# Stick-breaking weights by a product scan over keys, and a last output block handled in two pieces

## The chip, the cores and the metric

The kernel runs on one core of a Trainium2 chip. The metric is the device time of one execution in microseconds; lower is better. The engines are named as in the profile: PE is TensorE's matmul (PEld its weight load), DVE is VectorE, ACT is ScalarE, POOL is GpSimd, SP is SyncE, which issues most DMAs.

## The reference

Two layers of a hybrid block over 256 positions and width 1024, then a final RMSNorm. In each layer one projection feeds three branches, whose gated outputs are concatenated, projected and added to the residual:

- eight heads of dilated causal attention with rotary positions (A),
- a convolution and a gated linear recurrence (B),
- four heads of stick-breaking attention (C).

The change is in the third one and in the final norm. For one head and one block of queries:

```python
z = jnp.einsum('bhqd,bhkd->bhqk', q_blk, kf) * scale
causal = key_pos[None, :] < t[:, None]
log_keep = jnp.where(causal, jax.nn.log_sigmoid(-z), 0.0)
tail = lax.cumsum(log_keep, axis=3, reverse=True)
between = jnp.concatenate([tail[..., 1:], jnp.zeros_like(tail[..., :1])], axis=-1)
weights = jnp.where(causal, jnp.exp(jax.nn.log_sigmoid(z) + between), 0.0)
return jnp.einsum('bhqk,bhkd->bhqd', weights, vf)
```

A weight is thus sigmoid(z) of its key times the product of sigmoid(-z) over all later keys that are still before the query. The last step is `rms_norm(h, final_gain)`, where h has 1024 columns.

## The kernel before

All is held on the chip, 128 rows at a time. Weights come in chunks of 2048 columns, in two halves each, through five staging buffers `st`. A float32 number is split into a rounded high part (`whi`, by ACT, L103) and a rest (`wlo`, by DVE, L104), and each product is three matmuls (`mm3`, L207). Four chunks of split weights fit at a time. The order of the chunks is fixed: CH_CQ, CH_CK, CH_AQ[0], CH_AK[0], CH_BX, CH_AQ[1], CH_AK[1], CH_CG, CH_BG, CH_AG, then the output chunks. SP issues a half's DMA when its staging buffer is free, that is, when DVE has split the half that stood five halves ahead.

The instructions of PE stand in the order of the code, which was written out by hand; the other engines' orders are set by a scheduler when the program is built. Each engine runs its queue in order. Small jobs are put between the two column blocks of a projection: `proj_b(chunk, mid)` runs `mid` between them.

Stick-breaking attention before: `sb_scores` (in the middle of CH_AQ[0]) multiplies keys by queries, so that the keys lie on the partitions, with 256 queries for the first 128 keys and 128 for the second. It adds the mask with bfloat16 matmuls (`idb`, `cmb`). For each head, ACT and DVE make log(1 + e^z) from Abs, Exp, Ln, a maximum and a sum, and DVE splits that into `sh` and `sl`. `sb_weights` then sums over later keys with four matmuls a head against a triangular table `trir` (L397, L399), onto the scores themselves, and ACT takes Exp (L82) to `wv`. The four calls of `sb_weights` stand after blocks of CH_AK[0] and CH_BX. With the keys on the partitions, `values` (L358) can use `wv` at once. It writes the bank `y`, of which there is one.

The dilated attention has the queries on the partitions in its scores (L426); its probabilities are turned by PE (`dil_transposes`, L455) and copied by ACT to `wv` (L456). DVE's `emit_y` (L345) frees the `y` bank.

ACT's functions need tables: Exp and Ln are in one set, Sigmoid and Tanh in another, and a change of set is an instruction (L76).

At the end of layer 1, DVE adds each 512-column block of the output to the residual (L588). Then, for each of the two row blocks, ACT squares the two halves with a sum (L189), Ln and Exp give `rstd` (L82), DVE multiplies by the gain (L595), DVE and ACT scale one half each (L597, L599), and SP issues the output (L600).

Of the kernel before, what the change touches and what calls it, by code (L numbers as in the profile page):

```python
# [9 lines left out]
F32 = mybir.dt.float32  # L10
# [5 lines left out]
P = 128  # L16
# [12 lines left out]
AHEAD = 2  # L29
WST = 5  # L30
SCR = 7
WARM = 7

C_ID = 0
C_NM = 128
C_CM = 512
C_TRI = 640
C_W = 768
SM_P = 16
SM_W = 512  # L40
SHUF = list(range(8, 16)) + list(range(0, 8)) + list(range(16, 32))
# [6 lines left out]
def trunk_kernel(ctx: ExitStack, tc: tile.TileContext, x, first_x, first, wpack, prm_d, gatew, gains, consts, rope, out):  # L48
# [15 lines left out]
    def scr(w):  # L64
        return wk.tile([P, 512], F32, name="scr", tag="scr", bufs=SCR)[:, 0:w]

# [5 lines left out]

    loaded = {"load": None, "users": []}

    def table(name):
        load = act.preload_act_table_set(name)  # L76
        for u in loaded["users"]:
            dep(load, u)
        loaded["load"], loaded["users"] = load, []

    def tab(*a, **k):
        i = dep(act.activation(*a, **k), loaded["load"])  # L82
        loaded["users"].append(i)
        return i
# [7 lines left out]
    xh = sb.tile([P, NK, S], F32R, name="xh", tag="xh")  # L92
    xl = sb.tile([P, NK, S], F32R, name="xl", tag="xl")

    def load_chunk(l, c):
        hi = wsp.tile([P, 2048], F32R, name="whi", tag="whi")
        lo = wsp.tile([P, 2048], F32R, name="wlo", tag="wlo")
        for i in range(2):
            st = wst.tile([P, 1024], F32, name="st", tag="st")
            nc.sync.dma_start(out=st, in_=wpack[l, c][:, i * 1024:(i + 1) * 1024])  # L100
            for j in range(0, 1024, 512):
                ws, ss = slice(i * 1024 + j, i * 1024 + j + 512), slice(j, j + 512)
                act.activation(hi[:, ws], st[:, ss], AF.Copy)  # L103
                dve.tensor_sub(lo[:, ws], st[:, ss], hi[:, ws].bitcast(F32))  # L104
        return hi, lo

# [70 lines left out]

    tiny = cst.tile([P, 1], F32, name="tiny")
    dve.memset(tiny, 1e-19)
    trir = cst.tile([P, 2, P], F32R, name="trir")  # L180
    ones = cst.tile([P, P], F32, name="ones")
    dve.memset(ones, 1.0)
    idb = cst.tile([P, P], BF16, name="idb")
# [18 lines left out]
    def mm3(ps, lhs, rhs, ks, first, last):  # L202
        lh, ll = lhs
        rh, rl = rhs
        seq = [(a, b, k) for a, b in ((lh, rh), (lh, rl), (ll, rh)) for k in ks]
        for i, (a, b, k) in enumerate(seq):
            pe.matmul(ps, a(k), b(k), start=first and i == 0, stop=last and i == len(seq) - 1)  # L207

    def normed(t):
        rstd = rms_stats(t, gps)  # L210
# [50 lines left out]
    for l in range(L):  # L261
# [87 lines left out]
        def head(h):  # L349
            return slice((h % 2) * HD, (h % 2) * HD + HD), h // 2, slice(h * HD, (h + 1) * HD)  # L350
# [10 lines left out]

        qc = sb.tile([P, 2, S], F32, name="qc", tag="q1")
        kc = sb.tile([P, 2, S], F32, name="kc", tag="k1")
        zs, sp_hl = {}, {}

        def sb_scores():
            for p in (0, 2):
                for h in (p, p + 1):
                    zs[h] = bank(at, "s")
                for h in (p, p + 1):  # L370
                    hr, hb, _ = head(h)
                    pe.matmul(zs[h][:, 0:256], kc[hr, hb, 0:128], qc[hr, hb, :], start=True, stop=True)  # L372
                for h in (p, p + 1):
                    hr, hb, _ = head(h)
                    pe.matmul(zs[h][:, 256:384], kc[hr, hb, 128:256], qc[hr, hb, 128:256],  # L375
                              start=False, stop=True, skip_group_check=True)
            for h in range(NHC):
                for c in (0, 256):
                    pe.matmul(zs[h][:, c:c + 128], idb, cmb, start=False, stop=True, skip_group_check=True)  # L379
            for h in range(NHC):  # L380
                z = zs[h]
                e = scr(384)
# [3 lines left out]
                sp = scr(384)  # L386
                dve.scalar_tensor_tensor(sp, z[:, 0:384], 0.0, e, ALU.max, ALU.add)
                sh = wk.tile([P, 384], F32R, name="sh", tag="sh", bufs=3)
                sl = wk.tile([P, 384], F32R, name="sl", tag="sl", bufs=3)
                dve.tensor_copy(sh, sp)  # L390
                dve.tensor_sub(sl, sp, sh.bitcast(F32))
                sp_hl[h] = sh, sl

        def sb_weights(h):
            z = zs[h]
            for sv in sp_hl[h]:
                pe.matmul(z[:, 128:256], trir[:, 1, :], sv[:, 256:384], start=False, stop=True,  # L397
                          skip_group_check=True)
                pe.matmul(z[:, 0:384], trir[:, 0, :], sv, start=False, stop=True, skip_group_check=True)  # L399
            if h == 0:  # L400
                zs["w"] = wk.tile([P, 4, 384], F32, name="wv", tag="wv", bufs=1)
            tab(zs["w"][:, h, :], z[:, 0:384], AF.Exp)

        def rotate(ps, tiles, h0, tag):
            dst = tiles[h0] = sb.tile([P, 2, S], F32, name=tag, tag=tag)
# [5 lines left out]
            dve.tensor_mul(v2(sw), v2(sw), ss)  # L411
            dve.tensor_add(dst, dst, v2(sw))

        halves = ((0, slice(0, 128)), (1, slice(128, 384)))
        qT, kT = {}, {}
        prob = {}

# [29 lines left out]
                prob[h] = pr  # L447

        def dil_transposes(h0):
            pts = wk.tile([P, 12, P], F32, name="wv", tag="wv", bufs=1)  # L450
            for g in range(3):
                tp = bank(at, "s")
                for i in range(4):
                    h, j = divmod(4 * g + i, 3)
                    pe.transpose(tp[:, i * P:(i + 1) * P], prob[h0 + h][:, j * P:(j + 1) * P], ident)  # L455
                act.activation(pts[:, 4 * g:4 * g + 4, :].rearrange("p k c -> p (k c)"), tp, AF.Copy)  # L456
            return [pts[:, 3 * h:3 * h + 3, :].rearrange("p k c -> p (k c)") for h in range(4)]
# [49 lines left out]
        if l > 0:  # L507
            scaled(qc, cq_ps, 0.125)
        if l == 0:
            tri = scr(2 * P)  # L510
            nc.sync.dma_start(out=tri, in_=consts[:, C_CM:C_W])
            dve.tensor_copy(idb, ident)
            dve.tensor_copy(cmb, tri[:, 0:P])
            dve.tensor_copy(trir[:, 0, :], tri[:, P:2 * P])
            dve.tensor_scalar(trir[:, 1, :], ones, -1.0, None, ALU.mult)
        ck_ps = proj_b(CH_CK, rows_of_rstd if l == 0 else None)
        if l == 0:
            scaled(qc, cq_ps, 0.125)
# [2 lines left out]
            for i in range(2):  # L521
                dve.tensor_mul(rp0[:, i, :], rp[:, i, :], rb)
        rotate(proj_b(CH_AQ[0], sb_scores), qT, 0, "q0")
        rotate(proj_b(CH_AK[0], lambda: sb_weights(0)), kT, 0, "k0")
        sb_weights(1)
        conv(proj_b(CH_BX, lambda: sb_weights(2)))
        sb_weights(3)
        y_c = {}

        def second():  # L530
            y_c["y"] = values(vc, [zs["w"][:, h, :] for h in range(NHC)], 0)
            dil_softmax(dil_scores(0))

        rotate(proj_b(CH_AQ[1], second), qT, 4, "q1")
# [37 lines left out]
                if (t, n2) == (0, 1):  # L572
                    emit_y(values(va, y_c["p"], 4), ag[:, 2:4, :], 6, 2)
        if l > 0:
            gf = cst.tile([P, D], F32, name="gf", tag="gn")
        nc.sync.dma_start(out=gn if l == 0 else gf, in_=gains[l:l + 1, :].broadcast_to([P, D]))
        ow = [weights(l, CH_O + 2 + n2) for n2 in range(2)]
        for t in range(NT):
            if t == 1 and l == 0:
                next_x = [sb.tile([P, NK, S], F32R, name=n, tag=n) for n in ("xh", "xl")]  # L580
                xn0 = normed(0)
            for n2 in range(2):
                cs = slice(n2 * 512, n2 * 512 + 512)
                for ks in ((0, 1), (2, 3)):
                    out_mm(o_ps[t, n2], ow[n2], t, 1, ks, False, ks[0] == 2)
                    if (l, t, n2, ks[0]) == (0, 1, 1, 0):
                        turn(xn0, 0, *next_x)
                dve.tensor_add(xres[:, t, cs], o_ps[t, n2], xres[:, t, cs])  # L588

    for t in range(NT):  # L590
        rstd = rms_stats(t, gps)
        for half in range(2):
            cs = slice(half * 512, half * 512 + 512)
            ot = scr(512)
            dve.tensor_mul(ot, xres[:, t, cs], gf[:, cs])  # L595
            if half == 0:
                dve.tensor_scalar(ot, ot, rstd, None, ALU.mult)  # L597
            else:
                act.activation(ot, ot, AF.Copy, scale=rstd)  # L599
            nc.sync.dma_start(out=out[t * P:(t + 1) * P, cs], in_=ot)  # L600


def _shape_constants():
    f = np.float32
    con = np.zeros((P, C_W), f)
    con[:, C_ID:C_ID + P] = np.eye(P, dtype=f)
    nm = np.full((P, 384), -8 * BIG, f)
    for t0, c0, n in ((0, 0, 128), (128, 128, 256)):
        d = (t0 + np.arange(P))[:, None] - np.arange(n)[None, :]
        c = (d <= 128).astype(int) + (d % 4 == 0) + (d % 16 == 0)  # L610
        c = np.where(d >= 0, c, 0)
        nm[:, c0:c0 + n] = np.where(c > 0, 8 * np.log(np.maximum(c, 1).astype(np.float64)), -8 * BIG)
# [3 lines left out]
    con[:, C_TRI:C_TRI + P] = np.where(i[:, None] >= i[None, :], -1.0, 0.0)  # L616
    return con


# [89 lines left out]
```

## Time and profile before

| | |
|---|---|
| median of 3 runs | 254.09 us (253.51 to 254.46) |
| the profiled execution | 253.61 us |
| its span | 251.8 us |
| granted TensorE clock, mean | 0.995 |
| mean DMA rate | 173 GB/s |

The profile is of one execution. A row of the groups names line, engine and operation, what is written and read, how often, then busy us in all and mean ns of one, then the engine's idle time just before and what ended it. In a timeline or chain row the first two numbers are the start from the span's beginning and the length, both in us; "x6" says that six instructions are merged. Durations overlap a little on one engine, so starts tell the rate.

### The profile page before, as it was taken

To read this page: it belongs to the slowest core of one execution; us is meant where nothing else is said; L and a number is where in the kernel's file an instruction comes from. 1 tells how busy PE (TensorE), PEld (TensorE's weight loads), DVE (VectorE), ACT (ScalarE), POOL (GpSimd) and SP (SyncE) were. 2 spreads that over 40 slices of the span, in tenths; PEclk is the share of its full clock that TensorE was granted. 3 is DMA by queue.
4 is the path that set the end of the run, shared out by engine and by line. 5 is a ranking of instruction groups with operands and counts; after the bars stand their busy time and mean duration, and the time that the engine had idled before them with its cause. 6 is when DMAs were issued, how large, how long until landed. Compare 5 with 4: busy or idle time off the path is not lost.

```text
span 251.8 us, 4728 instructions
## 1 busy us (share of the span) xinstructions
PE 244.2 (97%) x1777; PEld 223.1 (89%) x1777; DVE 190.7 (76%) x429; ACT 163.9 (65%) x355; POOL 8.3 (3%) x33
## 2 busy tenths in 40 slices
PE   8999999999999999999999999999999999999990
PEld 4989999998999899878889999999899979987870
DVE  4874799999999589985792865399999856985253
ACT  3859969941947499964762864693394659993143
POOL 0037000000000000000000000000000000000000
PEclk9999999999999999999999999999999999999998
DMA  7989988923547631287175586540725732000022
GB/s 215 400 260 407 368 297 272 351 87 99 197 156 235 196 105 64 85 247 275 63 230 189 182 291 198 166 148 21 250 87 163 242 98 83 3 0 0 3 83 83
DMA packets 13126, 43.44 MB, mean 173 GB/s; under 512 B 1584, under 2 KB 2224, under 8 KB 13104
## 3 DMA queue, kind: packets, MB, share of 16 engines
q1 hardware_dynamic: 12816, 42.89, 50.4%
q8 instruction: 14, 0.23, 0.3%
q10 hardware_dynamic: 288, 0.26, 0.3%
q14 instruction: 8, 0.07, 0.1%
HBM read 42.09 MB, written 1.05 MB: 171 GB/s over the span
## 4 chain that ended last, share of the span: by engine, by line
PE 97%; ACT 1%; DVE 0%; issue 0%; ACTq 0%
PE pp L207 66%; PE s L207 9%; PE s L163 5%; PE y L358 3%; PE s L426 2%; PE pp L163 2%; PE s L455 2%; PE s L399 1%; PE pp L481 1%; PE y L134 1%; PE s L372 1%; PE s L223 1%; PE s L379 0%; PE s L397 0%; PE s L375 0%; ACT scr L189 0%
## 5 line engine op out<-in xcount | busy, mean ns | idle before, releaser
L104 DVE TENSOR_TENSOR wlo<-st,whi 128x512 fp32r<-128x512 f32 x132 | 84.5, 685 | 21.9 <-ACT whi L103 21.4
L103 ACT ACTIVATE whi<-st 128x512 fp32r<-128x512 f32 x132 | 74.3, 623 | 35.9 <-PE pp L207 17.2
L207 PE MATMUL pp<-xh,whi 128*128 128x256 f32 x352 | 50.0, 285 | 0.0
L207 PE MATMUL pp<-xl,whi 128*128 128x256 f32 x352 | 49.4, 283 | 0.0
L207 PE MATMUL pp<-xh,wlo 128*128 128x256 f32 x352 | 49.4, 283 | 0.0
L207 PEld LDWEIGHTS pp<-xh,whi 128*128 128x128 f32 x352 | 45.7, 191 | 1.3 <-issue 1.3
L207 PEld LDWEIGHTS pp<-xh,wlo 128*128 128x128 f32 x352 | 45.4, 192 | 0.0
L207 PEld LDWEIGHTS pp<-xl,whi 128*128 128x128 f32 x352 | 45.4, 192 | 0.0
L82 ACT ACTIVATE pr<-scr,mn 128x128 f32<-128x128 f32 (+1 forms) x32 | 14.1, 442 | 9.2 <-DVE mn L433 9.2
L189 ACT ACTIVATE scr<-xres 128x512 f32<-128x512 f32 x12 | 7.5, 627 | 13.4 <-DVE xres L588 12.9
L207 PE MATMUL pp<-whi,yh 128*128 128x512 f32 x48 | 14.1, 394 | 0.0
L207 PE MATMUL pp<-wlo,yh 128*128 128x512 f32 x48 | 13.8, 390 | 0.0
L207 PE MATMUL pp<-whi,yl 128*128 128x512 f32 x48 | 13.8, 389 | 0.0
L76 ACT ACT_TABLE_LOAD x9 | 11.5, 1283 | 1.8 <-PEq L702 1.6
L82 ACT ACTIVATE scr<-scr 128x384 f32<-128x384 f32 (+1 forms) x20 | 10.8, 539 | 0.5 <-DVE scr L324 0.3
L207 PEld LDWEIGHTS pp<-wlo,yh 128*128 128x128 f32 x48 | 9.0, 188 | 1.9
L207 PEld LDWEIGHTS pp<-whi,yl 128*128 128x128 f32 x48 | 9.0, 188 | 1.9
L207 PEld LDWEIGHTS pp<-whi,yh 128*128 128x128 f32 x48 | 8.7, 188 | 1.6
L346 ACT ACTIVATE yh<-scr 128x512 fp32r<-128x512 f32 x8 | 5.1, 633 | 7.6 <-DVE scr L345 7.5
L588 DVE TENSOR_TENSOR xres<-pp,xres 128x512 f32<-128x512 f32 x6 | 4.1, 689 | 7.3 <-PE pp L207 7.3
L433 DVE CUSTOM_DVE_ANT_0 scr<-s,con 128x128 f32<-128x128 f32 (+1 forms) x32 | 9.2, 354 | 0.6 <-PE s L426 0.6
L446 DVE TENSOR_SCALAR pr<-pr,den 128x128 f32<-128x128 f32 (+1 forms) x32 | 8.7, 315 | 0.3
(161 smaller groups left out, 347.5 us busy)
## 6 DMA issues: line engine op xcount, KB each, us to landing
st<-w_pack SPq DMA_DIRECT2D x66, 512.0 KB, 5.1
st<-first SPq DMA_DIRECT2D x7, 512.0 KB, 5.6
xres<-x_in SPq DMA_DIRECT2D x2, 512.0 KB, 8.2
out<-scr SPq DMA_DIRECT2D x4, 256.0 KB, 2.2
gw_t<-gate_w SPq DMA_DIRECT2D x2, 256.0 KB, 6.8
gn<-gains SPq DMA_DIRECT2D x1, 512.0 KB, 6.8
gf<-gains SPq DMA_DIRECT2D x1, 512.0 KB, 4.7
st<-first ACTq DMA_DIRECT2D x2, 128.0 KB, 3.4
```

The source lines that it names most:

```text
L76: load = act.preload_act_table_set(name)
L82: i = dep(act.activation(*a, **k), loaded["load"])
L103: act.activation(hi[:, ws], st[:, ss], AF.Copy)
L104: dve.tensor_sub(lo[:, ws], st[:, ss], hi[:, ws].bitcast(F32))
L163: pe.matmul(ps[t][:, c0 - base:c1 - base], a[:, k, t * P:(t + 1) * P], b[:, c0:c1], start=k == 0 and i == 0 and c0 == base, stop=k == NK - ...
L189: act.activation(scr(512), xres[:, t, i * 512:(i + 1) * 512], AF.Square, accum_out=sq[:, i:i + 1])
L207: pe.matmul(ps, a(k), b(k), start=first and i == 0, stop=last and i == len(seq) - 1)
L346: act.activation(yh[:, k0:k0 + n, :], dst, AF.Copy)
L358: pe.matmul(y[hr, p * 128 + o:p * 128 + 256], vt[:, s0, hs], wts[i][:, ws], start=s0 == 0, stop=s0 == 1)
L426: pe.matmul(sps[h][:, cs], qT[h0][hr, hb, t * P:(t + 1) * P], kT[h0][hr, hb, 0:(t + 1) * P], start=True, stop=True)
L433: dve.tensor_tensor_reduce(xs[:, cs], sps[h][:, cs], nmask[:, cs], -0.125, 3e38, ALU.add, ALU.min, mn[:, t:t + 1])
L446: dve.tensor_scalar(pr[:, cs], pr[:, cs], den[:, t:t + 1], None, ALU.mult)
```

## The change

Scores are made with the queries on the partitions. ACT makes two sigmoids a head, of z and of -z. DVE forms the product over later keys with a scan that runs backward over the keys (two scans a head, one for each block of queries), and multiplies. PE turns the weights in twelve 128 x 128 transposes a layer, in three groups, and ACT copies them to `wv`. The triangular table goes. ACT's table set is changed twice more in each layer. In the last layer, the addition for the last output block is made in two pieces of 320 and 192 columns; DVE sums the squares of the first piece and ACT those of the second; the final norm's steps move into `finish`, called behind each block; and the second half of each output is issued from ACT's queue in place of SP's.

```diff
+LATE = 320
-    def table(name):
+    def table(name, behind=()):
...
-        for u in loaded["users"]:
+        for u in (*loaded["users"], *behind):
...
+    def finish(t, n2):
+        ot = last["ot", t, n2] = scr(512)
+        x_t = xres[:, t, n2 * 512:n2 * 512 + 512]
...
+        if n2 == 0:
+            act.activation(scr(512), x_t, AF.Square, accum_out=sq[:, 0:1])
+            gps.tensor_scalar(ss, sq[:, 0:1], 1.0 / D, EPS, ALU.mult, ALU.add)
+            dve.tensor_mul(ot, x_t, last["gf"][:, 0:512])
+            return
+        c, late = 0, ss
+        if t == 1:
+            c, late = LATE, sq[:, 2:3]
+            dve.tensor_tensor_reduce(scr(c), x_t[:, 0:c], x_t[:, 0:c], 1.0 / D, ss, ALU.mult, ALU.add, late)
+        act.activation(scr(512 - c), x_t[:, c:512], AF.Square, scale=D ** -0.5, accum_out=sq[:, 1:2])
+        dve.tensor_mul(ot, x_t, last["gf"][:, 512:1024])
...
+        for half, queue in ((0, nc.sync), (1, act)):
...
+            queue.dma_start(out=out[t * P:(t + 1) * P, half * 512:half * 512 + 512], in_=o)
...
         def sb_scores():
...
-                    pe.matmul(zs[h][:, 0:256], kc[hr, hb, 0:128], qc[hr, hb, :], start=True, stop=True)
...
+                for t, cs in halves:
+                    for h in (p, p + 1):
+                        hr, hb, _ = head(h)
+                        pe.matmul(zs[h][:, cs], qc[hr, hb, t * P:(t + 1) * P], kc[hr, hb, 0:(t + 1) * P],
+                                  start=t == 0, stop=True, skip_group_check=True)
             for h in range(NHC):
                 for c in (0, 256):
-                    pe.matmul(zs[h][:, c:c + 128], idb, cmb, start=False, stop=True, skip_group_check=True)
+                    pe.matmul(zs[h][:, c:c + 128], cmb, idb, start=False, stop=True, skip_group_check=True)
+            table(SIGM, [split[l, CH_AK[0]]])
             for h in range(NHC):
...
-                act.activation(e, z[:, 0:384], AF.Abs)
-                tab(e, e, AF.Exp, scale=-1.0)
-                tab(e, e, AF.Ln, bias=1.0)
...
+                tab(om, z, AF.Sigmoid, scale=-1.0)
+                tab(bt, z, AF.Sigmoid)
+                w = sw[h] = wk.tile([P, 384], F32, name="sw", tag="sw", bufs=4)
+                gps.memset(w[:, 383:384], 0.0)
+                for lo, k0, k1 in ((0, 1, 128), (127, 128, 384)):
+                    n = k1 - k0
+                    dve.tensor_tensor_scan(w[:, lo:lo + n][:, ::-1], om[:, k0:k1][:, ::-1],
+                                           zero.broadcast_to([P, n]), 1.0, ALU.mult, ALU.add)
+                dve.tensor_mul(w, bt, w)
...
+        def turned(tiles, h0, gs, to):
+            for g in gs:
+                tp = bank(at, "s")
+                for i in range(4):
+                    h, j = divmod(4 * g + i, 3)
+                    pe.transpose(tp[:, i * P:(i + 1) * P], tiles[h0 + h][:, j * P:(j + 1) * P], ident)
+                act.activation(to[:, 4 * g:4 * g + 4, :].rearrange("p k c -> p (k c)"), tp, AF.Copy)
...
-        rotate(proj_b(CH_AK[0], lambda: sb_weights(0)), kT, 0, "k0")
-        sb_weights(1)
-        conv(proj_b(CH_BX, lambda: sb_weights(2)))
-        sb_weights(3)
+        rotate(proj_b(CH_AK[0]), kT, 0, "k0")
+        sw_t = turned_tile()
+        conv(proj_b(CH_BX, lambda: turned(sw, 0, (0,), sw_t)))
+        turned(sw, 0, (1, 2), sw_t)
...
+            table(LN_EXP)
             dil_softmax(dil_scores(0))
...
+                parts = ((0, LATE), (LATE, 512)) if l > 0 and (t, n2) == (1, 1) else ((0, 512),)
```

`split` remembers the last ACT split of each chunk, so that the table load stands behind the splits of CH_AK[0].

The order of instructions moves on three engines. On PE in layer 0, from the projection of CH_AK[0] through CH_BX to CH_AQ[1], each row is eight projection matmuls (L207) or one triangular matmul. Before, at the end of CH_AK[0] and the start of CH_BX:

```order
L207 MATMUL pp<-xh,wlo 128x256 x8
L397 MATMUL s<-sh,trir 128x128
L399 MATMUL s<-sh,trir 128x384
L397 MATMUL s<-sl,trir 128x128
L399 MATMUL s<-sl,trir 128x384
L207 MATMUL pp<-xh,whi 128x256 x8
```

That group stands four times in a layer. In the changed program, CH_BX's two blocks (now L210) and what follows, with the transposes at L433:

```order
L433 MATMUL s<-con,sw 128x128 x4
L210 MATMUL pp<-xh,whi 128x256 x8
L210 MATMUL pp<-xl,whi 128x256 x8
L210 MATMUL pp<-xh,wlo 128x256 x8
L433 MATMUL s<-con,sw 128x128 x8
L210 MATMUL pp<-xh,whi 128x256 x8
```

The four groups of triangular matmuls have become two groups of transposes, in the middle of CH_BX and behind it, and CH_AK[0] runs without a break.

On DVE in layer 0, behind the scores. Before (L387, L390 and L391 are the steps of a head, L104 the splits):

```order
L104 TENSOR_TENSOR wlo<-st,whi 128x512 x7
L387 SCALAR_TENSOR_TENSOR scr<-s,scr 128x384
L104 TENSOR_TENSOR wlo<-st,whi 128x512
L390 CAST sh<-scr 128x384
L104 TENSOR_TENSOR wlo<-st,whi 128x512
L391 TENSOR_TENSOR sl<-scr,sh 128x384
L104 TENSOR_TENSOR wlo<-st,whi 128x512
L387 SCALAR_TENSOR_TENSOR scr<-s,scr 128x384
L104 TENSOR_TENSOR wlo<-st,whi 128x512
```

In the changed program, from the third head's second scan on; L424 is the scans (shown under the name SCALAR_TENSOR_TENSOR), L426 the product, L106 the splits, L447 to L450 the rotation behind CH_AQ[0]:

```order
L424 SCALAR_TENSOR_TENSOR sw<-scr,zero 128x256
L424 SCALAR_TENSOR_TENSOR sw<-scr,zero 128x127
L426 TENSOR_TENSOR sw<-scr,sw 128x384
L424 SCALAR_TENSOR_TENSOR sw<-scr,zero 128x256
L447 STREAM_SHUFFLE scr<-pp 128x512
L426 TENSOR_TENSOR sw<-scr,sw 128x384
L448 TENSOR_TENSOR q_656<-pp,rp_297 128x512
L449 TENSOR_TENSOR scr<-scr,rp_297 128x512
L106 TENSOR_TENSOR wlo<-st,whi 128x512
L450 TENSOR_TENSOR q_656<-q_656,scr 128x512
L106 TENSOR_TENSOR wlo<-st,whi 128x512 x2
```

The splits that stood between the steps of a head now stand behind all four heads' scans; six splits stand directly ahead of the first one.

On ACT in layer 0, from the scores to the first dilated softmax (`pr`). Before, the last three Exp to `wv` and splits:

```order
L82 ACTIVATE wv<-s 128x384
L103 ACTIVATE whi<-st 128x512
L82 ACTIVATE wv<-s 128x384
L103 ACTIVATE whi<-st 128x512 x4
L82 ACTIVATE wv<-s 128x384
L82 ACTIVATE pr,den<-scr,mn 128x128
```

In the changed program, with the sigmoids at L82 and the copies of the turned weights at L434:

```order
L105 ACTIVATE whi<-st 128x512 x12
L76 ACT_TABLE_LOAD
L105 ACTIVATE whi<-st 128x512 x6
L82 ACTIVATE scr<-s 128x384 x8
L105 ACTIVATE whi<-st 128x512 x6
L76 ACT_TABLE_LOAD
L105 ACTIVATE whi<-st 128x512 x4
L434 ACTIVATE wv<-s 128x512
L105 ACTIVATE whi<-st 128x512 x3
L434 ACTIVATE wv<-s 128x512 x2
L105 ACTIVATE whi<-st 128x512
L82 ACTIVATE pr,den<-scr,mn 128x128
```

The second and third copies to `wv` stand behind three of the four splits of CH_BG; before, the last Exp stood behind all four.

More of the change, by code (lines that the diff above doesn't have):

```diff
@@ L385, in sb_scores @@
-                tab(e, e, AF.Ln, bias=1.0)
[L386 to L402, printed above, removed]
+                z = zs[h][:, 0:384]
@@ L404, in rotate, with by_head @@
+        def by_head(pts):
+            return [pts[:, 3 * h:3 * h + 3, :].rearrange("p k c -> p (k c)") for h in range(4)]
         def rotate(ps, tiles, h0, tag):
```

77 lines of the change are left out of this document (36 added, 41 removed).

## The prediction

> **What bounds the kernel now.** I read the page's shares first, then the chain that ended last, then what each engine waited for, and last the timeline around the two changed places.
>
> ```profile
> span 251.8 us, 4728 instructions
> PE 244.2 (97%) x1777; PEld 223.1 (89%) x1777; DVE 190.7 (76%) x429; ACT 163.9 (65%) x355; POOL 8.3 (3%) x33
> ...
> DVE  4874799999999589985792865399999856985253
> ```
>
> The third row is the page's strip of 40 slices.
>
> ```profile
> PE 97%; ACT 1%; DVE 0%; issue 0%; ACTq 0%
> ```
>
> ```profile
> PE y L134 <- DVE cold L122: 1.2, 1, 1.2
> ```
>
> The chain is TensorE for 97% of the span, and the only wait that PE has is the first one, 1.2 us. From there to the last matmul PE never starves, so a matmul taken out before the end moves the end by its whole length, as long as nobody makes PE wait. The strip says where that could happen: VectorE (DVE) has eight nines in a row, from 31 to 82 us, which is layer 0's attention. There it has almost no air, and it feeds PE (splits), SP (freed weight buffers) and the y bank.
>
> **Term 1, PE.** The rows are the chain in order of time (start, length).
>
> ```profile
> 39.62 5.81 PE pp L207 x48
> ...
> 46.00 2.88 PE pp L207 x24
> ...
> 49.45 2.88 PE pp L207 x24
> ...
> 52.90 2.88 PE pp L207 x24
> ...
> 56.34 2.87 PE pp L207 x24
> 59.21 1.45 PE y L358 x16
> ...
> 79.63 1.31 PE s L455 x12
> 80.94 1.73 PE pp L481 x8
> ...
> 159.94 5.81 PE pp L207 x48
> ...
> 179.53 1.45 PE y L358 x16
> ```
>
> From 39.62 to 59.21 are 19.59 us, of which the projections take 5.81 + 3 x 2.88 + 2.87 = 17.32. The four triangular groups between them are the remaining 2.27 us. Layer 1 has the same 19.59 from 159.94 to 179.53, so 4.54 us go in all. What comes is twelve transposes a layer, of the form of L455: twelve stand in 1.31 us. Two layers are 2.62 us. The scores keep their column count, 128 + 256 a head, and the mask keeps its eight matmuls with the operands exchanged, so I count no difference there. Net: 2.62 - 4.54 = -1.92 us, if PE stays fed.
>
> ```profile
> L455 PE MATMUL s<-con,pr 128*128 128x128 f32 x48 | 5.9, 272 | 0.0
> ```
>
> One transpose lasts 272 ns, but they overlap: the chain's row gives 0.109 us each, and I take that. The Trainium skill, TensorE: Matmul & The Clock Gate, Part 4: PE-mode transpose, puts a transpose at about 275 ns in one kernel. Charged like that, 24 would be 6.6 us and the PE term +2.1 us, a loss; this trace has that duration and not that spacing.
>
> **Term 2, DVE and ScalarE (ACT): what has to stay hidden.** Groups by line, with shapes kept apart:
>
> ```profile
> L387 DVE SCALAR_TENSOR_TENSOR scr<-s,scr 128x384 f32<-128x384 f32 x8 | 4.4, 553 | 3.7 <-ACT scr L82 3.7
> L390 DVE CAST sh<-scr 128x384 fp32r<-128x384 f32 x8 | 2.8, 352 | 0.1
> L391 DVE TENSOR_TENSOR sl<-scr,sh 128x384 fp32r<-128x384 f32 x8 | 4.4, 554 | 0.1
> L501 DVE TENSOR_TENSOR_SCAN rt<-av,it 128x256 f32<-128x256 f32 x4 | 2.5, 678 | 0.0
> L522 DVE TENSOR_TENSOR rp<-rp,rb 128x256 f32<-128x256 f32 x2 | 0.8, 418 | 0.0
> L82 ACT ACTIVATE scr<-scr 128x384 f32<-128x384 f32 x16 | 8.3, 519 | 0.3
> L456 ACT ACTIVATE wv<-s 128x512 f32<-128x512 f32 x12 | 6.3, 594 | 1.1 <-PE s L455 1.1
> L76 ACT ACT_TABLE_LOAD x9 | 11.5, 1283 | 1.8 <-PEq L702 1.6
> ```
>
> ```profile
> 37.11 3.69 DVE L104 TENSOR_TENSOR wlo<-st,whi 128x512 fp32r<-128x512 f32 x6
> 96.76 1.27 DVE L501 TENSOR_TENSOR_SCAN rt<-av,it 128x256 f32<-128x256 f32 x2
> ```
>
> Back to back, DVE starts the next instruction about 0.09 us before the old one's end: two scans take 1.27 and not 1.36, six splits 3.69, so 0.60 each. A head costs now 0.47 + 0.27 + 0.47 = 1.21 us of DVE. After: a scan over 256 columns, 0.59; one over 127, which no row shows; and a product over 384, 0.47 (as L391). A 256 scan takes what a 512-wide elementwise takes, so I price the 127 one like a 256-wide elementwise, 0.33 (0.42 less overlap); the ends are 0 and 0.59. No row has a scan through reversed addresses or with a constant second operand; I take the forward price, since that is the same instruction, and the doubled one is a rival below. Sum 1.39, that is 0.18 more a head and 0.72 us more a layer.
>
> ACT loses four activations a head (some 0.5 us each) and gets two sigmoids: eight fewer a layer, 4 us. Three copies and two table loads a layer take that back, 3 x 0.59 + 2 x 1.28 = 4.3 us. It is level, and ACT has a third of its time free. The DVE memset and cast that change, and four memsets of one column on POOL (3% busy), lie under waits.
>
> What is queued behind what is the real question, since the order moves more than the work: all eight scans now stand ahead of the splits that used to stand between the old steps. In layer 0 two chains come close to PE.
>
> (a) There are five staging buffers, so SP issues a half chunk only when DVE has split the one five halves ahead: the second half of CH_BG waits for the second split of CH_AK[1]. Behind the third split of CH_BG stand, on ACT's queue, the last two copies of transposed weights, for which PE's first value products wait.
>
> ```profile
> L100 SPq DMA_DIRECT2D st<-w_pack x1: 327/327/327, 55.8 to 55.8; - x1
> ...
> DMA to landing us min/median/max: 3.7/3.7/3.7
> ```
>
> DVE is free at 40.72 (37.11 + 3.69 less overlap). Four heads, 5.56; then eleven 512-wide operations up to the second split of CH_AK[1], at 0.60, 6.6: done at 52.97. A single transfer on an idle queue lands after 3.7 (this row is the one at 55.8): 56.7. One split on ACT (0.52 with overlap) and a copy (0.59): the second copy is there at 57.8, the third at 58.3. PE gets there at 39.62 + 17.32 + 0.44 + 0.87 = 58.25, and needs the third copy half of 1.45 us later, 58.97. Air: 0.4 us.
>
> (b) The y bank is single. PE's second value products wait for DVE's product of y with cg.
>
> ```profile
> 80.56 0.69 DVE L345 TENSOR_TENSOR scr<-y,cg 128x512 f32<-128x512 f32 x1
> ```
>
> ```profile
> 82.60 1.52 PE L358 MATMUL y<-wv,va 128*64 128x256 f32 x16
> ```
>
> ```profile
> DVE wlo L104 <- PE pp L207: 0.4, 1, 0.4
> ```
>
> Before, 81.25 against 82.60, air 1.35. After, PE comes 0.96 earlier, 81.64, and DVE 0.72 later less the 0.4 idle that it loses: 81.57. As many splits stand ahead of it as before. Air: 0.1 us. Layer 1 has more: the 3.7 us of idle in L387's row is there, ahead of its first head. I charge 0.1 us for (a) and (b) together; the ends are 0 and, if the DVE prices are a quarter too low (1.4 us a layer), 1.3.
>
> **Term 3, the tail.** The rows are timeline rows after the last matmul.
>
> ```profile
> 245.39 0.69 DVE L588 TENSOR_TENSOR xres<-s,xres 128x512 f32<-128x512 f32 x1 [2.03 <-PE s L207]
> 246.11 0.63 ACT L189 ACTIVATE scr<-xres 128x512 f32<-128x512 f32 x1 [1.99 <-DVE xres L588]
> 246.65 0.19 ACT L189 ACTIVATION_READ_ACCUMULATOR scr<-xres 128x1 f32 x1
> 246.93 0.29 ACT L82 ACTIVATE lnv<-sq,ss 128x1 f32<-128x1 f32 x1
> 247.49 0.72 ACT L599 ACTIVATE scr<-scr,rstd 128x512 f32<-128x512 f32 x1
> 248.00 0.81 SPq L600 DMA_DIRECT2D out<-scr  x2
> ```
>
> ```profile
> L433 DVE CUSTOM_DVE_ANT_0 scr<-s,con 128x256 f32<-128x256 f32 x16 | 6.7, 420 | 0.0
> ```
>
> Two additions, of 320 and 192 columns, end 0.75 us after their start where one took 0.69 (0.49 less 0.09, plus 0.35): +0.06. ACT's square then has 192 columns in place of 512. L82's 384 columns and L456's 512 differ by 0.075 us, so 320 columns are 0.19 less; the ends are 0.1 and 0.3. The square runs 0.54 us now before its accumulator is read, and the logarithm starts 0.28 after that. DVE's square over 320 columns, like L433 at 420 ns plus 64 columns, 0.49, starts 0.67 after the first addition's start and is read out by 1.2, ahead of the logarithm at 1.41 (now 1.54). DVE's product with the gain follows, done at 1.8, and the scale waits until 1.97 for rstd. So 0.13 us to there. The last output goes to ACT's queue and doesn't wait for SP, which issues two in 0.81: the second began some 0.2 us after its data were ready. Together -0.33; the ends are 0 (later landing from ACT's queue, no gain in the square) and -0.5.
>
> **Sum.** -1.92 + 0.1 - 0.33 = -2.15 us. The profiled execution took 253.61 (span 251.8 and 1.8 around it) and would take 251.5. It lies 0.48 below the median of the runs, 254.09, so for a median I say 251.9.
>
> **Rivals.**
> 1. Slower: the reversed scans cost twice the forward row. Place: DVE in layer 0 from 40.72 on. Then 4 x 0.92 = 3.7 us more, chain (a) makes PE wait 3.3, and layer 1 between 0 and 3.3 in the same way: 254.09 - 2.3 + 3.3 to 6.6, 255.1 to 258.4. It decides from 2.25 + 0.4 = 2.65 us over four heads, scans at 1.7 times the row. For it: DVE is full there, and no row has the form. Against: the same instruction and width.
> 2. Part of the gain is lost in chain (a): the transfer lands after 5.1 us, the median of all 66, instead of 3.7, or DVE is 1 to 1.5 us later. PE waits 0.9 to 1.3: 252.8 to 253.2.
>
> ```profile
> st<-w_pack SPq DMA_DIRECT2D x66, 512.0 KB, 5.1
> ```
>
>    Against: nothing else is in the queue then.
> 3. The twelve transposes cost 272 ns each, because they don't overlap here: 24 x 0.272 = 6.5 against 4.54, +2.0 - 0.3: 255.8. The chain's row speaks against it. The Trainium skill's price, named above, is this rival's.
> 4. The tail changes nothing, since the landing decides: 252.3.
>
> **How the numbers follow.** From no change I can tell about 0.5%, 1.27 us. Forecast with air or a few tenths lost: 0.62 (faster). Rival 4: 0.08 (faster). Rival 2: 0.18, of which half stays over 1.27 us. Rival 1: 0.07 (slower), rival 3: 0.02 (slower). The rest, 0.03, is no change. So faster 0.79, same 0.12, slower 0.09. The range goes from 250.9 (no wait, the tail's full 0.5, and runs like the fastest shown, 0.6 under the median) to 253.6 (rival 2 whole, and a little of the runs' spread); it leaves out rivals 1 and 3.
>
> **What would show it.** Right: the chain still all PE, transposes of 0.44 and 0.87 us where the triangular groups stood, values some 0.96 and 1.92 us earlier in the two layers, scans of 0.68 and 0.42 us, no new PE wait over 0.3 us, and the last output issued by ACT. Wrong: a wait of PE before the value products (L358 now) for ACT's copy or DVE's product, scans over 1 us, or a longer stretch from the last matmul to the end than 6.4 us.

## The result and the profile after

| | before | after |
|---|---|---|
| median of the runs | 253.58 us (20 runs, 253.0 to 255.3) | 252.27 us (20 runs, 251.24 to 253.69) |
| ratio, with 95% interval | | 0.9939 [0.992, 0.9958] |
| the profiled execution | 253.61 us, span 251.8 | 252.72 us, span 250.7 |

Faster by 0.6%, between 0.4 and 0.8%: 1.5 us, where 2.15 were forecast. A second set of runs of the same two kernels gave 251.42 against 253.46, ratio 0.9914 [0.9895, 0.9933], that is 2.2 us. So the size is known to about half a microsecond from the times; the profiles are finer.

The page of the changed kernel and, below it, shares and rows of the chain that ended last (start, length; some rows between them left out):

```profile
span 250.7 us, 4730 instructions
PE 242.5 (97%) x1769; PEld 221.2 (88%) x1769; DVE 191.9 (77%) x431; ACT 164.1 (65%) x349; POOL 9.4 (4%) x41
```

```profile
0.72 3.66 DMA x<-first_x
...
7.94 0.82 PE s L165 x4
...
23.68 8.64 PE pp L210 x72
...
40.58 11.57 PE pp L210 x96
52.16 0.44 PE s L433 x4
52.59 2.87 PE pp L210 x24
55.47 0.87 PE s L433 x8
56.34 2.86 PE pp L210 x24
59.20 1.45 PE y L393 x16
...
159.94 11.57 PE pp L210 x96
171.51 0.44 PE s L433 x4
...
178.56 1.45 PE y L393 x16
...
241.68 2.73 PE s L210 x12
```

From the end of the mask (40.58) to the value products (59.20) are 18.62 us where 19.59 stood before, and the same in layer 1 (159.94 to 178.56). Where the triangular matmuls were are transposes of 0.44 and 0.87. From the first projection row, 72 matmuls at 23.68, to the last matmul's end, 244.41, are 220.73 us. In the profile before that row began at 22.72 and the last matmul ended at 245.36: 222.64. So PE does the program 1.91 us faster, but in this execution it began it 0.96 us later. The list of what PE waited for shows the same:

```profile
PE y L136 <- DVE cold L124: 1.2, 1, 1.2
PE s L165 <- ACT xh L149: 0.7, 1, 0.7
```

The first line is that of before; the second is new, stands in the first microseconds, and its cause is the chain's first row: `first_x` landed after 3.7 us, where it took 3.0 before, so that the first matmul on loaded data began at 5.04 and not at 4.34. That is 0.70 of the 0.96 us. The other 0.26 lie in the matmuls that follow: they stood at about double spacing for longer than before, four in 0.82 us still at 7.94, where the chain of before had come down by then:

```profile
7.32 0.47 PE s L163 x4
```

No later matmul waited for anything that this view shows.

VectorE's new steps in layer 0 (groups by line, shapes apart):

```profile
L424 DVE TENSOR_TENSOR_SCAN sw<-scr,zero 128x256 f32<-128x256 f32 x4 | 2.7, 685 | 0.0
L426 DVE TENSOR_TENSOR sw<-scr,sw 128x384 f32<-128x384 f32 x4 | 2.2, 539 | 0.0
L424 DVE TENSOR_TENSOR_SCAN sw<-scr,zero 128x127 f32<-128x127 f32 x4 | 1.6, 404 | 0.0
```

A scan read backward costs 685 ns for 256 columns; the forward one in the profile before cost 678. The place of chain (a), ACT's timeline and then PE's:

```profile
57.66 0.63 ACT L105 ACTIVATE whi<-st 128x512 fp32r<-128x512 f32 x1 [1.55 <-DMA st<-w_pack]
58.19 1.07 ACT L434 ACTIVATE wv<-s 128x512 f32<-128x512 f32 x2
```

```profile
59.13 1.52 PE L393 MATMUL y<-wv,vc 128*64 128x256 f32 x16
```

ACT waited for the half chunk, split it, and then made the two copies; the first of them was there at about 58.7, 0.4 us ahead of PE. And chain (b), VectorE and PE:

```profile
81.23 0.70 DVE L380 TENSOR_TENSOR scr<-y,cg 128x512 f32<-128x512 f32 x1
```

```profile
82.59 1.52 PE L393 MATMUL y<-wv,va 128*64 128x256 f32 x16
```

The product ends at 81.93, some 0.7 us ahead. The end, after the last matmul (timeline), and the two queues' outputs:

```profile
244.44 0.76 DVE L622 TENSOR_TENSOR xres<-s,xres 128x320 f32<-128x320 f32 x2 [1.30 <-PE s L210]
245.11 0.54 DVE L229 CUSTOM_DVE_ANT_0 scr<-xres,ss 128x320 f32<-128x320 f32 x1
245.22 0.36 ACT L230 ACTIVATE scr<-xres 128x192 f32<-128x192 f32 x1 [2.06 <-DVE xres L622]
...
246.36 0.72 ACT L241 ACTIVATE scr<-scr,rstd 128x512 f32<-128x512 f32 x1
246.83 0.34 SPq L242 DMA_DIRECT2D out<-scr  x1
247.11 0.35 ACTq L242 DMA_DIRECT2D out<-scr  x1
```

```profile
out<-scr SPq DMA_DIRECT2D x2, 256.0 KB, 2.1
out<-scr ACTq DMA_DIRECT2D x2, 256.0 KB, 2.5
```

ACT's scale begins 1.92 us after the addition's start, where it was 2.10 (245.39 to 247.49). The last output leaves 0.75 us after that (0.94 before), but a store needs 2.5 us to land from ACT's queue and 2.1 from SP's (medians of two).

So this one pair of profiles gives 0.96 - 1.91 - 0.15 at the end (spans are given to 0.1 us), and leaves two questions. Is the later start the change's doing? And why does the run take 2.0 us more than its span (252.72 less 250.7), where before it was 1.8?

### The profile page after: what moved, and what is told of

It is laid out like the page before. It is cut to its first block, busy times and chain, and to the rows that moved or that the text cites. A ratio compares the mean times of both kernels' runs of the same rounds, so it can differ in the third digit from the quotient of the medians.

```text
span 250.7 us, 4730 instructions
## 1 busy us (share of the span) xinstructions
PE 242.5 (97%) x1769; PEld 221.2 (88%) x1769; DVE 191.9 (77%) x431; ACT 164.1 (65%) x349; POOL 9.4 (4%) x41
## 4 chain that ended last, share of the span: by engine, by line
PE 95%; DMA 1%; ACT 1%; DVE 0%; issue 0%; ACTq 0%
PE pp L210 66%; PE s L210 9%; PE s L165 5%; PE y L393 3%; PE s L433 3%; PE pp L165 2%; PE s L463 2%; DMA x<-first_x 1%; PE pp L513 1%; PE s L409 1%; PE s L258 1%; PE s L413 0%; DVE xres L622 0%; ACT scr L241 0%; ACT xh L149 0%; ACT scr L230 0%
## 5 line engine op out<-in xcount | busy, mean ns | idle before, releaser
L106 DVE TENSOR_TENSOR wlo<-st,whi 128x512 fp32r<-128x512 f32 x132 | 84.2, 689 | 20.4 <-ACT whi L105 20.4
L210 PE MATMUL pp<-xh,whi 128*128 128x256 f32 x352 | 50.3, 285 | 0.0
L210 PE MATMUL pp<-xh,wlo 128*128 128x256 f32 x352 | 49.4, 283 | 0.0
L210 PE MATMUL pp<-xl,whi 128*128 128x256 f32 x352 | 49.4, 283 | 0.0
L210 PEld LDWEIGHTS pp<-xh,whi 128*128 128x128 f32 x352 | 45.2, 191 | 1.3 <-issue 1.3
L210 PEld LDWEIGHTS pp<-xh,wlo 128*128 128x128 f32 x352 | 45.4, 192 | 0.0
L210 PEld LDWEIGHTS pp<-xl,whi 128*128 128x128 f32 x352 | 45.4, 192 | 0.0
L82 ACT ACTIVATE pr<-scr,mn 128x128 f32<-128x128 f32 (+1 forms) x32 | 14.1, 443 | 7.9 <-DVE mn L470 7.9
L210 PE MATMUL pp<-whi,yh 128*128 128x512 f32 x48 | 14.1, 394 | 0.0
L210 PE MATMUL pp<-wlo,yh 128*128 128x512 f32 x48 | 13.8, 390 | 0.0
L210 PE MATMUL pp<-whi,yl 128*128 128x512 f32 x48 | 13.8, 389 | 0.0
L434 ACT ACTIVATE wv<-s 128x512 f32<-128x512 f32 x18 | 9.6, 593 | 4.6 <-PE s L433 4.6
L210 PEld LDWEIGHTS pp<-wlo,yh 128*128 128x128 f32 x48 | 9.0, 188 | 1.9
L210 PEld LDWEIGHTS pp<-whi,yl 128*128 128x128 f32 x48 | 9.0, 188 | 1.9
L210 PEld LDWEIGHTS pp<-whi,yh 128*128 128x128 f32 x48 | 8.7, 188 | 1.6
L424 DVE TENSOR_TENSOR_SCAN sw<-scr,zero 128x127 f32<-128x127 f32 (+1 forms) x16 | 8.0, 544 | 2.6 <-ACT scr L82 2.6
L82 ACT ACTIVATE scr<-s 128x384 f32<-128x384 f32 x16 | 6.3, 522 | 5.1 <-PE s L413 5.1
```

The source lines that it names most:

```text
L424: dve.tensor_tensor_scan(w[:, lo:lo + n][:, ::-1], om[:, k0:k1][:, ::-1], zero.broadcast_to([P, n]), 1.0, ALU.mult, ALU.add)
L434: act.activation(to[:, 4 * g:4 * g + 4, :].rearrange("p k c -> p (k c)"), tp, AF.Copy)
```

## Experiments

The diffs are against the changed kernel unless said otherwise. Where the expectations speak of the "first 48-matmul projection" they mean the row of 72 just read.

**The change's parts, apart.** Four kernels shared 20 runs of the kernel before (median 253.46).

The changed kernel again: 

> The changed kernel once more, unchanged. In its first profile PE went through the program 1.91 us faster from the first 48-matmul projection on (220.73 against 222.64 us), but reached that projection 0.96 us later (23.68 against 22.72). Theory A (the later start is chance of the loads at the beginning): the stretch from that projection to the last matmul is 220.7 again within 0.1, the beginning lies anywhere from 22.5 to 23.8. Theory B (the change makes the start later): the projection begins at 23.5 or later again.

The new attention with the old tail (`finish` and the two pieces taken back): 

> The new attention alone, with the old tail. By the sum of the prediction: 1.92 us of PE go, 0.1 come back, so 1.8 us faster than before (ratio 0.993), and PE's stretch from the first 48-matmul projection to the last matmul 220.7 us. Theory B with the cause in the attention part (one memset more, constants 128 columns shorter): projection at 23.5 or later, and only about 0.9 us faster (0.9965).

The new tail on the old kernel: 

> The new tail alone, with the old attention. By the prediction's third term 0.33 us faster than before; by the profile of the changed kernel, where the last output landed late from ACT's queue, 0.15 us; the two can only be told by the profile: from the last matmul to the end of the span 6.1 us (prediction), 6.3 (late landing), against 6.44 before. Theory B with the cause in the tail: 48-matmul projection at 23.5 or later and the kernel 0.6 us or more slower than before.

Both outputs on SP:

```
-            for half, queue in ((0, nc.sync), (1, act)):
+            for half, queue in ((0, nc.sync), (1, nc.sync)):
```

> The changed kernel with both halves of each output on SP's queue. If ACT's queue lands later (2.43 us there, 2.05 on SP's in the first profile), the last output is issued 0.2 to 0.4 us later but lands in 2.0 to 2.3: last matmul to end 6.2 to 6.4, level with the change. If ACT's queue is no slower by itself, this is 0.2 to 0.4 us worse: 6.5 to 6.7.

Measured, with two kernels of the next part added. Start is that of the first 72-matmul row, PE from there to the last matmul's end, tail from the last addition's start to the end of the span, and outside is run time less span, mean over the runs:

| kernel | ratio to before | start | PE | tail | outside |
|---|---|---|---|---|---|
| before | | 22.72 | 222.64 | 6.4 | 1.78 |
| the change | 0.9939 [0.992, 0.9958] | 23.68 | 220.73 | 6.3 | 2.05 |
| again | 0.9914 [0.9895, 0.9933] | 22.95 | 221.79 | 6.2 | 2.07 |
| new attention, old tail | 0.9947 [0.9925, 0.9968] | 22.48 | 220.73 | 6.5 | 2.06 |
| old attention, new tail | 1.0004 [0.9986, 1.0022] | 22.43 | 222.64 | 6.2 | 1.80 |
| both outputs on SP | 0.9912 [0.9893, 0.993] | 22.37 | 220.73 | 6.2 | 2.06 |
| zeros by VectorE, outputs on SP | 0.9915 [0.99, 0.9931] | 22.35 | 220.78 | 6.2 | 1.79 |
| constants of 768, outputs on SP | 0.9941 [0.9922, 0.996] | 22.29 | 220.72 | 6.3 | 2.08 |

Five things follow.

1. PE's term is the attention's, and it repeats to a few hundredths in all profiles of this table but one: 222.64 with the old, 220.72 to 220.78 with the new. The one is the second profile of the change, where 221.79 came. There the first projection row took 9.59 us in place of 8.64, because its weight loads waited for ACT's splits (one of three such rows):

```profile
29.09 0.30 PEld L210 LDWEIGHTS pp<-xh,whi 128*128 128x128 f32 x2 [0.22 <-ACT whi L105]
```

   Another 0.10 went in layer 0's first value products, at the place of chain (a): there the first of ACT's two copies ended at about 59.41, just after PE had begun. Without these two, it is 220.74 again.

```profile
58.83 1.07 ACT L434 ACTIVATE wv<-s 128x512 f32<-128x512 f32 x2
```

```profile
59.35 1.62 PE L393 MATMUL y<-wv,vc 128*64 128x256 f32 x16
```

2. The start is chance. The kernel with both outputs on SP is the changed one in every instruction up to the tail, and it began at 22.37; the new attention alone at 22.48; the unchanged change at 23.68 in one execution and at 22.95 in the other. Theory B, which had 23.5 or later again, falls. A late `first_x` is not the whole of it: with constants of 768 the first matmul on loaded data came at 4.83, later than in before, and the row began at 22.29. There the double spacing had ended by 6 us, in the change only by 8.8. The granted clock is given as 1.00 in both stretches, so what ends it is not known from these views. The spans of before spread as widely (250.8 to 253.0 in 20 runs), but only one of its executions has a profile.
3. The tail gives 0.2 us. The times of the tail alone can't show that (1.0004, interval of 0.36%); the profiles can, if the tail is counted from the last addition's start to the end of the span: 251.8 - 245.39 = 6.41 before and 6.46 with the new attention alone; 6.26 and 6.23 in the change, 6.20 with the tail alone, 6.17, 6.24 and 6.26 with SP. Each is good to 0.05 us, so there are two values, one for the old tail and one for the new. The three with SP are the point: with SP the last output is issued 0.15 us later after ACT's scale (0.90 against 0.75) and lands in at most 2.3:

```profile
L242 SPq DMA_DIRECT2D out<-scr x4: 332/363/425, 240.4 to 246.0; - x4
...
DMA to landing us min/median/max: 2.0/2.2/2.3
```

   So ACT's queue gives nothing; the whole tail gain is the split square.
4. Outside the span the new attention costs 0.28 us. In all 45 runs of this table's kernels with POOL setting the zeros the difference lies between 2.00 and 2.12, and in every run of the old attention whose span is on record between 1.74 and 1.84. No view of the span shows it.
5. The parts add up to -1.91 - 0.2 + 0.28 = -1.83 us, and both ratios of the change (-1.5 and -2.2, each give or take 0.5) hold that.

**What the 0.28 us is.** Constants as wide as before and the zeros set by VectorE:

```
-                gps.memset(w[:, 383:384], 0.0)
+                dve.memset(w[:, 383:384], 0.0)
-C_W = 640
+C_W = 768
```

> For the 0.28 us that the new attention adds outside the span (run time less span: 1.78 with the old attention, 2.06 with the new, in every run): the changed kernel with the column of zeros set by VectorE in place of POOL, and the constants 768 columns wide as before. If POOL's eight instructions or the size of the constants cause it, 1.78; if it lies elsewhere (table loads, scans), 2.06.

Run time less span was 1.76 (253.06 less 251.3), so it is one of the two. Then each alone, with both outputs on SP. Zeros by VectorE: 

> The changed kernel with both output halves on SP's queue and the column of zeros set by VectorE in place of POOL; constants 640 columns wide as in the change. If POOL's eight instructions are what adds 0.28 us outside the span, run time less span is 1.78 and the kernel 0.3 us faster than with the outputs on SP alone (ratio to before 0.990, from 0.9912). If it is the width of the constants, run time less span stays 2.06 and the ratio at 0.991. VectorE gets eight one-column instructions of 0.06 us, which lie in chain (b)'s air of 0.75: no PE wait.

The width alone: 

> The changed kernel with both output halves on SP's queue and the constants 768 columns wide as before the change (the last 128 loaded and not used); POOL sets the zeros as in the change. The other way round: run time less span 1.78 if the width is the cause, 2.06 if POOL's instructions are.

Outside the span: 1.76 to 1.82 in six runs with VectorE, 2.04 to 2.10 in six with the wide constants and POOL. It is POOL's eight instructions. Last, four of the eight:

```
-                gps.memset(w[:, 383:384], 0.0)
+                (gps if l == 0 else dve).memset(w[:, 383:384], 0.0)
```

> Zeros by POOL in layer 0 only (four instructions, at POOL's beginning), by VectorE in layer 1. Run time less span was 2.06 with eight POOL instructions and 1.79 with none. If the price is per instruction, 1.93; if a step at some length of POOL's program, 1.79 or 2.06, the same for both layers; if only the early ones count, 2.06 here and 1.79 in the other.

> Zeros by POOL in layer 1 only (four instructions, in the middle of POOL's program). Per instruction 1.93; a step in the program's length: the same as in the other; only late ones count: 2.06 here and 1.79 in the other.

1.82 (250.92 less 249.1) and 1.79 (251.29 less 249.5), in one run each: not per instruction, and not by place. The page counts POOL's instructions as 33 with no zeros, 41 with eight, and 37 with four:

```profile
PE 241.6 (97%) x1769; PEld 220.2 (88%) x1769; DVE 191.9 (77%) x435; ACT 164.4 (66%) x349; POOL 9.3 (4%) x37
```

Somewhere between the two is a step of 0.28 us. That it hangs on the length of POOL's program fits all these runs; what the chip does in it was not found.

The kernel with zeros by VectorE and outputs on SP is the fastest that the parts point to: the same PE stretch, no 0.28 outside. Its times don't set it apart: the ratio is 0.9915, the change has 0.9939 and 0.9914, and the kernel with outputs on SP and zeros by POOL 0.9912. The 0.28 us is seen in run time less span alone.

**The cover of VectorE.** The first rival and both chains rest on how much more VectorE could bear. The scans done twice:

```
-                    dve.tensor_tensor_scan(w[:, lo:lo + n][:, ::-1], om[:, k0:k1][:, ::-1],
-                                           zero.broadcast_to([P, n]), 1.0, ALU.mult, ALU.add)
+                    for _ in range(2):
+                        dve.tensor_tensor_scan(w[:, lo:lo + n][:, ::-1], om[:, k0:k1][:, ::-1],
+                                               zero.broadcast_to([P, n]), 1.0, ALU.mult, ALU.add)
```

> The changed kernel with each scan done twice, the second over the first: 0.59 + 0.32 us more VectorE a head, 3.65 a layer, which is what the first rival charged. If chain (a) is what the prediction says, with 0.4 us of air, PE waits about 3.3 us in layer 0 ahead of its first value products, for the copy that stands behind the third split of CH_BG; layer 1 has 2 us of air and gives 0 to 1.6. In all 254.7 to 256.3 where the change takes 251.4. If instead VectorE has hidden slack there (the other theory), PE waits less than 1 us and the time stays within 1 us of the change.

With six staging buffers (`WST = 6`) and scans twice: 

> The same with six staging buffers in place of five. The second half of CH_BG then waits for the buffer that five would free three us earlier (50.99 and not 54.03 in the first profile of the change). If the prediction's chain (a) is right in its link over the staging buffer, PE's wait ahead of the first value products shrinks from 3.3 to under 0.5 us. VectorE is still 3.65 us late, so chain (b) is next: PE's second value products then wait for VectorE's product y x cg, 0.75 us of air against 3.65, so 2.5 to 2.9 us. Total only 0.4 to 0.8 us below the run with five buffers. If the staging buffer is not the link (the wait comes directly from VectorE), nothing changes at the first place.

Only the first head's scans twice (`range(2 if h == 0 else 1)`): 

> The changed kernel with only the first head's scans done twice: 0.91 us more VectorE in layer 0. With 0.4 us of air in chain (a) PE waits 0.5 us before the first value products, and nowhere else; with air over 0.9 it does not wait at all.

All shared ten runs of before (median 254.22). Scans twice: 257.25, ratio 1.0126 [1.0077, 1.0176]. With six buffers: 256.76, 1.0089 [1.0046, 1.0133]. One head, one run: 253.38. Scans twice is thus 3.0 us above before and 5 to 6 above the change (252.27 and 251.42), where 3.3 to 4.9 was expected. The size is a little more than that, and 1.4 us of it in the profiled execution is another thing, a slower clock (see the last section); the place is not as expected. What PE waited for, scans twice:

```profile
PE y L393 <- DVE scr L380: 2.8, 1, 2.8
...
PE y L393 <- ACT wv L435: 1.1, 2, 0.8
```

The long wait is in chain (b), for the product that frees the `y` bank, and not in (a). By starts on PE, from the first to the second value products in layer 0 it took 27.27 us where the change takes 23.46: 0.92 lost at (a), 2.89 at (b). The reason is in ACT's order, which the scheduler made anew when the scans cost more. Each row is a group of ACT's queue. The change and, below, scans twice:

```
L105 ACTIVATE whi<-st 128x512 x3
L434 ACTIVATE wv<-s 128x512 x2

L105 ACTIVATE whi<-st 128x512 x2
L435 ACTIVATE wv<-s 128x512 x2
```

Only two splits stand ahead of the copies, so they no longer wait for the second half of CH_BG, only for the first. The rest of VectorE's delay went on to (b), where it grew: the late splits freed a staging buffer late, ACT waited for the transfer, and VectorE for ACT's sigmoid (timeline of ACT, then of VectorE):

```profile
81.08 1.15 ACT L105 ACTIVATE whi<-st 128x512 fp32r<-128x512 f32 x2 [1.81 <-DMA st<-w_pack]
```

```profile
82.78 0.69 DVE L376 TENSOR_TENSOR cg<-scr 128x512 f32<-128x512 f32 x1 [1.26 <-ACT scr L82]
83.39 0.69 DVE L106 TENSOR_TENSOR wlo<-st,whi 128x512 fp32r<-128x512 f32 x1
83.99 0.69 DVE L380 TENSOR_TENSOR scr<-y,cg 128x512 f32<-128x512 f32 x1
```

Six buffers keep the old order of three splits. By the same count of starts PE lost 0.5 us at (a) and 1.9 at (b), where 2.5 to 2.9 was expected: with the extra buffer VectorE had no idle ahead of the product, and the transfer no longer adds to (b). Layer 1 lost 1.4 us in both, for a copy that stands behind ACT's part of `emit_y`:

```profile
PE y L393 <- DVE scr L380: 1.9, 1, 1.9
...
PE y L393 <- ACT wv L435: 0.8, 1, 0.8
```

One head, 0.91 us of VectorE: no wait at (a) (the scheduler took two splits here too, so this run can't tell (a)'s air), and 0.3 at (b), so that (b) bears 0.5 to 0.6 us:

```profile
83.24 1.52 PE L393 MATMUL y<-wv,va 128*64 128x256 f32 x16 [0.31 <-DVE scr L380]
```

The chain (a) with ACT's order of the change held fast and the scans doubled was not tried: with five buffers the scheduler gave another order each time.

## Why the prediction was right, and where not

**Term 1, PE: right.** -1.92 was forecast, -1.91 came, and the term repeated in every kernel, once the two late pieces of the second profile are taken out. The transposes cost their spacing, not their duration. The group of the change is

```profile
L433 PE MATMUL s<-con,sw x24: 272/272/273, 52.0 to 175.4; 128*128 128x128 f32 x24
```

and 24 of them took 2 x (0.44 + 0.87) = 2.62 us on the chain. Rival 3 and the Trainium skill's figure (TensorE: Matmul & The Clock Gate, Part 4: PE-mode transpose, about 275 ns) taken as a price are both off: the trace has that number as a duration only.

**Term 2, VectorE and ACT: the price right, one air wrong.** A head costs 5.47 / 4 = 1.37 us of VectorE (four heads from 41.77 to 47.87, less 0.63 for a shuffle that stands between), 1.39 forecast; rival 1's condition, scans at 1.7 times the row, is refuted by 685 against 678 ns. The 0.1 us charged for the two chains was not spent in the first profile, and just spent in the second. Chain (a)'s air came as worked out, 0.4, in the first; over the nine profiles of the new attention with single scans it lies between 0.44 and -0.06 us, so 0.4 is one draw of it.

Chain (b)'s air did not come as worked out, 0.7 in place of 0.1. The count behind it holds: as many splits stand ahead of the product after as before, 47 from the start of the program in both. The groups up to that product, before and after:

```profile
L104 DVE TENSOR_TENSOR wlo<-st,whi 128x512 fp32r<-128x512 f32 x47 | 30.3, 685 | 5.4 <-ACT whi L103 4.9 <-PE pp L207 0.4
```

```profile
L106 DVE TENSOR_TENSOR wlo<-st,whi 128x512 fp32r<-128x512 f32 x47 | 30.1, 691 | 4.0 <-ACT whi L105 4.0
```

What was mis-sized is what the old heads and the old idle time had cost. The steps of the third head of before stand directly behind each other, without splits between them, and took 1.53 us, not 1.21; the four took 5.14 and not 4.84. And VectorE idled twice around the heads, 0.16 and 0.45 us, where 0.4 was counted; after, it has no such idle there.

```profile
40.96 0.69 DVE L104 TENSOR_TENSOR wlo<-st,whi 128x512 fp32r<-128x512 f32 x1 [0.16 <-ACT whi L103]
...
46.99 0.55 DVE L387 SCALAR_TENSOR_TENSOR scr<-s,scr 128x384 f32<-128x384 f32 x1
47.57 0.36 DVE L390 CAST sh<-scr 128x384 fp32r<-128x384 f32 x1
47.97 0.56 DVE L391 TENSOR_TENSOR sl<-scr,sh 128x384 fp32r<-128x384 f32 x1
48.97 0.69 DVE L104 TENSOR_TENSOR wlo<-st,whi 128x512 fp32r<-128x512 f32 x1 [0.45 <-PE pp L207]
```

These are 0.30 and 0.21 us; with the new heads' 5.47 in place of 5.56 they make the 0.6 by which the air was larger.

**Rival 1's mechanism** had the price of 3.65 us and the total about right (255.1 to 258.4; scans twice took 257.25), but named chain (a) as the place, with ACT's order taken as fixed. The runs show (b) for most of it, and 1.4 us in layer 1; that the total fits is in part luck, since 1.4 us more in the profiled execution is a slower clock, which the rival doesn't have. Rival 2's waits of 0.9 to 1.3 us did not occur; its place showed once, with the 0.10 us of the second profile. Rival 4's 252.3 is the median of the 20 runs by chance: the tail did change.

**Term 3, the tail: half wrong.** -0.33 was forecast, -0.2 came. The split square was undersized (-0.13 forecast to rstd; 1.92 against 2.10, -0.18, measured): ACT's square of 192 columns ran 0.28 us before its accumulator was read, 0.26 less than the 0.54 of before, where 0.19 less was taken. ACT's queue was worth -0.2 in the forecast: the issue did come 0.19 earlier after the scale, and the landing took it back, 2.5 us against at most 2.3 on SP's.

**A term was missing.** "Four memsets of one column on POOL, lie under waits" is true inside the span, and "1.8 around it" was carried over as a constant. Those eight instructions made it 2.06. This 0.28 us, with the 0.13 of the tail, less the 0.1 not spent, is the difference of 0.3 between the forecast of -2.15 and the -1.83 of the parts.

**The median.** 251.9 was forecast from a base of 254.09, the median of three runs; twenty runs put it at 253.58. That base was 0.5 too high. From the lower base the parts give 251.75; the 20 runs of the change have 252.27 and the six later ones 251.42, on both sides of it, as a start that varies would make them. That 251.9 came so near to 252.27 is luck in part: a base 0.5 too high and a gain 0.3 too large lie on opposite sides.

## What to carry to other kernels

When one engine is the whole chain, what is taken out of it comes off in full, and can be priced to a few hundredths by starts in the chain; the time of a run is much coarser than that, so read a small term from its own stretch of the profile, counted from a start that chance doesn't move. Price a run as span plus what lies around it, and check that second part after every change, even one that adds only idle engines' instructions. Air on a full engine takes a count of what stands ahead in the built order on both sides, and prices and idle time read at the very place, for all heads and not for one; a what-if about it holds only while the scheduler leaves that order alone. One profile shows one draw of it.

## What the runs showed of the hardware

- An idle PE can come back at half its clock. With scans twice, PE stood still for 2.8 us, and its next 16 value products took 2.83 us in place of 1.52; the columns after the stretch are us, busy time and instructions of PE, PEld, DVE, ACT and POOL, then granted clock, DMA share and GB/s:

```profile
81.00:84.80 3.80, 1.00 (x5) 0.55 (x4) 2.54 (x5) 3.21 (x7) 0.00 (x0) 0.95 0.83 299
84.80:87.70 2.90, 2.88 (x18) 1.94 (x18) 2.15 (x4) 2.79 (x7) 0.00 (x0) 0.50 0.58 199
```

  With six buffers PE stood still for 1.9 us there, and in the profiled execution the clock stayed:

```profile
83.70:85.30 1.60, 1.58 (x18) 1.25 (x20) 1.60 (x3) 1.60 (x5) 0.00 (x0) 1.00 0.94 346
```

  So that wait cost 2.9 + 1.4 us (from the second to the third value products 28.52 us, in the change 27.11). In the four runs the mean clock was 0.985 and 0.987 with spans of 255.7 and 256.2, and 0.992 and 0.993 with 254.3 and 254.7: the half clock seems to come in some executions only. With six buffers too, three of the seven runs had 0.986 to 0.988 with spans of 254.7 to 256.1, the other four 0.992 to 0.994 with 253.0 to 255.0; so the shorter wait may not be safe, though no profile shows one of the three. The Trainium skill (TensorE: Matmul & The Clock Gate, Part 1) has the clock fall to half after an idle window of about 3.4 us that runs freely; here 2.8 us sufficed in the profiled execution.
- The same store of 256 KB lands after 2.4 to 2.5 us from ACT's queue and 2.0 to 2.3 from SP's.
- A step of 0.28 us outside the span between 37 and 41 instructions on POOL.
